# Full-row transposes of x with zeros below the samples, strip 6 transposed inside strip 7, and the last means by token tile

## The chip, the cores and the metric

The kernel runs on one core of a Trainium2 chip. The engines are TensorE (PE; its weight loads are listed apart as PEld), VectorE (DVE), ScalarE (ACT), GpSimd (POOL) and SyncE (SP), which here only issues transfers. The metric is the device time of one execution in microseconds (us), as the median of the runs.

## The reference, cut to what matters

One step of a hybrid streaming encoder in float32, for 256 prompt tokens and 64 sample tokens, each with 2048 features (320 tokens in all):

```
z    = x @ w_in                                   # 2048 -> 7184
mix  = concat(head_rms_norm(attention(z)), head_rms_norm(mLSTM(z)) * sigmoid(o)) @ w_out
x1   = layer_norm(ALPHA * x + mix, ln1_g, ln1_b)
ffn  = (silu(x1 @ w_ffn_gate) * (x1 @ w_ffn_up)) @ w_ffn_down      # 2048 -> 5632 -> 2048
y    = layer_norm(ALPHA * x1 + ffn, ln2_g, ln2_b)
```

layer_norm takes mean and variance of a token over its 2048 features, eps 1e-5. y is an output, tokens in rows. The caches and states that are outputs too lie outside the change.

## The kernel before

**Layout.** Activations are held with features in partitions and tokens in columns: 16 tiles of 128 features by T = 320 tokens. x arrives with tokens in rows, so TensorE transposes it first. `load_x` (L83) brings a quarter q of x (512 features) into a tile `xq` of 128 x 3 x 512: index 0 and 1 of the middle axis hold the 256 prompt tokens, index 2 holds the 64 sample tokens in rows 0 to 63; rows 64 to 127 of it stay as they are. `transpose_x` (L212) makes three transposes for each of the four feature tiles of a quarter, by the list `TOK = [(0, 128), (128, 128), (256, 64)]` of token tiles: the third has 64 rows. Three transposes fill one PSUM tile `w`; ScalarE casts it into a high part `xhi` (L218), VectorE subtracts to get a low part `xlo` (L219).

**Products.** Each weight is cut into a high and a low part too (`split_piece`, L115: ScalarE L130, VectorE L131), and a product is three matmuls: high weight by low x (L180), high by high (L181), low by high (L183). A *strip* is 256 output features, a *piece* is up to four feature tiles by 256 columns of a weight (512 KB). `run_plan` (L158) walks through the list `plan` of pieces; for each of the two 128-column halves of a piece it calls a hook, if one is stored under (piece, half), and then issues the matmuls. A strip's `done` function runs behind its last piece. `spawn` stores a generator that `advance` steps once per piece. The order on each engine is chosen by the framework's scheduler, except for the first eight pieces with the transposes of x (`manual_schedule`) and for instructions given to `keep_in_program_order`. In the first stretch the transposes of quarter 0 stand ahead of piece 0 and of piece 1, quarter 1 ahead of the second half of piece 3, quarter 2 ahead of that of piece 5, quarter 3 ahead of that of piece 7.

**The end.** The last product is `w_ffn_down`, in six groups of up to eight feature tiles; the sixth has four, so a strip there is one piece, two halves of twelve matmuls. `down_done` (L906) adds a strip to the tile y (L912). In the last group each strip but the last also spawns `stat_gen` (L786): six transposes of the strip's two feature tiles back to token rows (L795, 128 columns wide for the two prompt token tiles, 64 wide for the samples), three statistics on VectorE (L797), copies to `ytp` and `yts` by ScalarE (L800, L801), and there a multiplication by the second norm's gain on GpSimd (L803, L805). The generator starts one strip late, so strip 6 is transposed behind strip 7's matmuls; strip 7 follows at once. Then `norm_stats` (L824) joins the statistics to mean and variance, `norm_rsqrt` (L829 to L838) takes the inverse root in small steps on three numbers a row, L1057 to L1065 build a tile `c5` of five columns for each token tile from minus mean times inverse root, TensorE transposes it (L1068), ScalarE casts the three results at once to `r5` (L1070), and twelve matmuls with the gain and bias rows `g5` (L1077), each followed by one VectorE operation (L1078) and a store (L1080), finish y in 512-column parts. The transposes and these twelve share four PSUM tiles `w`.

Of the kernel before, what the change touches and what calls it, by code (L numbers as in the profile page):

```python
# [10 lines left out]
F32R = mybir.dt.float32r  # L11
I32 = mybir.dt.int32
AF = mybir.ActivationFunctionType
ALU = mybir.AluOpType
# [6 lines left out]
P = 128  # L21
DM = 2048
KT = DM // P
SP = 256
SS = 64
T = SP + SS
# [36 lines left out]
def _build(tc, nc, I, O, es):  # L63
# [9 lines left out]
    def w_tile():  # L73
        return pp.tile([P, 512], F32, tag="w", bufs=4, name="w")
# [4 lines left out]
    xq = []  # L79
# [3 lines left out]
    def load_x(q, c0=0, c1=512):  # L83
        if c0 == 0:
            xq.append(big.tile([P, 3, 512], F32, tag="Ba" if q < 2 else "Bb", bufs=2, name="xq"))
        t = xq[q]
        nc.sync.dma_start(out=t[:, 0:2, c0:c1], in_=xp[:, :, q * 512 + c0:q * 512 + c1])
        if c0 == 0:
            nc.sync.dma_start(out=t[0:SS, 2, :], in_=xs[:, q * 512:(q + 1) * 512])
# [47 lines left out]
    def spawn(gen, delay=0):  # L137
        active.append([gen, delay])
# [73 lines left out]
    def transpose_x(q, k0=0, k1=4):  # L212
        for kk in range(k0, k1):
            k = q * 4 + kk
            ps = w_tile()
            for i, (t0, n) in enumerate(TOK):
                TE.transpose(ps[:, t0:t0 + n], xq[q][0:n, i, kk * P:(kk + 1) * P], ident[0:n, 0:n])  # L217
            S.copy(xhi[:, k, :], ps[:, 0:T])  # L218
            V.tensor_tensor(out=xlo[:, k, :], in0=ps[:, 0:T], in1=xhi[:, k, :].bitcast(F32),  # L219
                            op=ALU.subtract)  # L220
# [566 lines left out]
    def stat_gen(s, keep):  # L787


        y, st = late["y"], late["st"]  # L790
        pa, pb = w_tile(), w_tile()
        dst = (pa[:, 0:256], pa[:, 256:512], pb[0:SS, 0:256])
        for j, (t0, n) in enumerate(TOK):
            for i in range(2):
                TE.transpose(dst[j][:, i * P:(i + 1) * P], y[:, 2 * s + i, t0:t0 + n], ident)  # L795
        for j, (t0, n) in enumerate(TOK):
            V.bn_stats(st[0:n, j, s, :], dst[j])  # L797
        if keep is not None:
            cs = slice(s * 256, (s + 1) * 256)
            S.copy(keep[0][:, :, cs], pa.rearrange("p (n c) -> p n c", c=256))  # L800
            S.copy(keep[1][:, cs], dst[2])  # L801
            for j in range(2):
                G.tensor_tensor(out=keep[0][:, j, cs], in0=keep[0][:, j, cs], in1=late["g2"][:, cs],  # L803
                                op=ALU.mult)
            G.tensor_tensor(out=keep[1][:, cs], in0=keep[1][:, cs], in1=late["g2"][0:SS, cs],  # L805
                            op=ALU.mult)
        return
        yield
# [95 lines left out]
    NG = (FT + 7) // 8  # L904

    def down_done(g, s, ps):  # L906
        y = late["y"]
        if g == NG - 1 and s == 0:
            sqrt_table(ps[0][:, 0:1])
        for i in range(2):  # L910
            c = 2 * s + i
            V.scalar_tensor_tensor(out=y[:, c, :], in0=y[:, c, :], scalar=ALPHA if g == 0 else 1.0,  # L912
                                   in1=ps[i][:, 0:T], op0=ALU.mult, op1=ALU.add)
        if g == NG - 1:
            if s == 0:
                late["ytp"] = big.tile([P, 2, DM], F32, tag="A", bufs=2, name="ytp")
                late["yts"] = big.tile([SS, DM], F32, tag="A", bufs=2, name="yts")
            if s < 7:
                spawn(stat_gen(s, (late["ytp"], late["yts"])), 1)

    def gate_up(u):
        rhs = yg_rhs if u < 2 else x1_rhs
# [9 lines left out]
    def down(g):  # L932
        nk = min(8, FT - g * 8)

        def rhs(k):
            return hbuf[("h", g)][:, k, :], hbuf[("l", g)][:, k, :]
        for s in range(8):
            add_strip(I["w_ffn_down"][g * 8 * P:(g * 8 + nk) * P, :], s * 256, 256, rhs,
                      lambda ps, s=s: down_done(g, s, ps), krows=nk)

    for g in range(NG):
        for u in range(g * 4, min(g * 4 + 4, FT // 2)):
            gate_up(u)
        if g > 0:
            down(g - 1)
    down(NG - 1)


    load_x(0, 0, 256)
# [101 lines left out]
    with tc.high_priority():  # L1051
        for _ in stat_gen(7, (late["ytp"], late["yts"])):
            pass
        mv = norm_stats()
        rn = norm_rsqrt(mv)
        nb = lp.tile([P, 3], F32, name="nb")
        V.scalar_tensor_tensor(out=nb, in0=mv[:, :, 0], scalar=-1.0, in1=rn,  # L1057
                               op0=ALU.mult, op1=ALU.mult)

        c5 = lp.tile([P, 3, 5], F32, name="c5")  # L1060
        G.memset(c5, 1.0)
        nbh = lp.tile([P, 3], F32R, name="nbh")
        V.tensor_copy(nbh, nb)
        S.copy(c5[:, :, 0:2], nb.unsqueeze(2).to_broadcast([P, 3, 2]))
        V.tensor_tensor(out=c5[:, :, 2], in0=nb, in1=nbh.bitcast(F32), op=ALU.subtract)  # L1065
        ps = w_tile()
        for j in range(3):
            TE.transpose(ps[0:5, j * P:(j + 1) * P], c5[:, j, :], ident)  # L1068
        r5 = lp.tile([5, 3, P], F32R, name="r5")
        S.copy(r5, ps[0:5, 0:3 * P].rearrange("p (n c) -> p n c", c=P))  # L1070
    for j, (t0, n) in enumerate(TOK):
        v = late["ytp"][:, j, :] if j < 2 else late["yts"]
        dst = O["y_prompt"][t0:t0 + n, :] if j < 2 else O["y_sample"]
# [42 lines left out]
```

## Time and profile before

| | us |
|---|---|
| median of 3 runs (1577.54 to 1581.7) | 1580.44 |
| the profiled execution's own time | 1577.66 |
| its span | 1575.9 |
| TensorE busy | 1561.3 |
| VectorE busy | 835.6 |
| ScalarE busy | 632.4 |
| GpSimd busy | 106.9 |

The profile is of one execution. A row of time order gives the start in us from the span's beginning, the length in us, the engine, the line, the operation with output and inputs, and how many neighbours were merged; in brackets stands the engine's idle time before it and what ended it. A row of a group gives the busy time and the mean of one in ns.

### The profile page before, as it was taken

What the parts mean: (1) busy time and instruction counts of PE and PEld (TensorE: products, weight loads), DVE (VectorE), ACT (ScalarE), POOL (GpSimd) and SP (SyncE); (2) the same over time, 40 slices, a digit from 0 to 9 for tenths busy, and PEclk for the clock granted to TensorE, in tenths of its full rate; (3) what the DMA queues carried; (4) which work ended last, traced back from release to release, by engine and by line L of the source; (5) the groups of instructions that cost most, each with busy time, mean ns of one, the idle gap of its engine ahead of it and who ended that gap; (6) DMA issues with size and microseconds to landing.
All of it is one profiled execution on the core that took longest, in us unless ns stands there. A gap on an engine that the chain in (4) does not pass through costs nothing.

```text
span 1575.9 us, 26646 instructions
## 1 busy us (share of the span) xinstructions
PE 1561.3 (99%) x10924; PEld 1544.1 (98%) x10924; DVE 835.6 (53%) x1529; ACT 632.4 (40%) x969; POOL 106.9 (7%) x249
## 2 busy tenths in 40 slices
PE   9999999999999999999999999999999999999997
PEld 8999999999999999999999999999999999999995
DVE  4486575665865655853344433444335443444456
ACT  4466444454445443643333233323333333333332
POOL 4013101110100000000000000000000000000004
PEclk9999999999999999999999999999999999999997
DMA  8545454444445444445555554444544444444442
GB/s 272 154 147 168 144 161 140 142 150 139 120 136 172 150 147 141 140 148 164 176 162 170 160 162 152 152 147 147 149 153 153 148 147 148 151 148 156 147 134 68
DMA packets 226011, 239.01 MB, mean 152 GB/s; under 512 B 8827, under 2 KB 220475, under 8 KB 225627
## 3 DMA queue, kind: packets, MB, share of 16 engines
q1 hardware_dynamic: 220944, 223.90, 46.0%
q0 software_dynamic: 4944, 13.40, 2.6%
q8 instruction: 86, 1.41, 0.4%
q14 instruction: 37, 0.30, 0.1%
HBM read 230.85 MB, written 10.07 MB: 153 GB/s over the span
## 4 chain that ended last, share of the span: by engine, by line
PE 98%; DVE 1%; issue 0%; ACT 0%; DVEq 0%
PE mm L180 31%; PE mm L181 30%; PE mm L183 30%; PE w L439 1%; PE w L795 1%; PE w L217 1%; PE w L395 0%; PE w L462 0%; PE w L962 0%; PE w L419 0%; DVE ytp L1078 0%; PE w L372 0%; PE w L422 0%; PE w L378 0%; PE w L397 0%; PE w L622 0%
## 5 line engine op out<-in xcount | busy, mean ns | idle before, releaser
L131 DVE TENSOR_TENSOR lo<-raw,hi 128x1024 fp32r<-128x1024 f32 (+1 forms) x410 | 499.0, 1218 | 578.7 <-ACT hi L130 578.2
L130 ACT CAST hi<-raw 128x1024 fp32r<-128x1024 f32 (+1 forms) x410 | 428.3, 1045 | 725.9 <-PE mm L181 636.1
L183 PE MATMUL mm<-x1h,lo 128*128 128x320 f32 (+1 forms) x1408 | 435.5, 309 | 0.0
L181 PE MATMUL mm<-x1h,hi 128*128 128x320 f32 (+1 forms) x1408 | 435.0, 309 | 0.0
L180 PE MATMUL mm<-x1l,hi 128*128 128x320 f32 (+1 forms) x1408 | 434.9, 309 | 0.0
L180 PE MATMUL mm<-xlo,hi 128*128 128x320 f32 x912 | 287.2, 315 | 1.0 <-DVE xlo L219 1.0
L181 PE MATMUL mm<-xhi,hi 128*128 128x320 f32 x912 | 280.7, 308 | 0.0
L183 PE MATMUL mm<-xhi,lo 128*128 128x320 f32 x896 | 277.2, 309 | 0.7 <-DVE lo L131 0.7
L183 PEld LDWEIGHTS mm<-x1h,lo 128*128 128x128 f32 x1408 | 265.3, 188 | 0.0
L180 PEld LDWEIGHTS mm<-x1l,hi 128*128 128x128 f32 x1408 | 265.0, 188 | 0.1
L181 PEld LDWEIGHTS mm<-x1h,hi 128*128 128x128 f32 x1408 | 264.8, 188 | 0.0
L180 PE MATMUL mm<-hl,hi 128*128 128x320 f32 x704 | 218.0, 310 | 0.0
L183 PE MATMUL mm<-hh,lo 128*128 128x320 f32 x704 | 217.6, 309 | 0.0
L181 PE MATMUL mm<-hh,hi 128*128 128x320 f32 x704 | 217.5, 309 | 0.0
L180 PEld LDWEIGHTS mm<-xlo,hi 128*128 128x128 f32 x912 | 171.3, 188 | 1.8 <-ACT hi L130 1.2
L181 PEld LDWEIGHTS mm<-xhi,hi 128*128 128x128 f32 x912 | 171.4, 188 | 0.0
L183 PEld LDWEIGHTS mm<-xhi,lo 128*128 128x128 f32 x896 | 168.2, 188 | 1.2 <-DVE lo L131 1.2
L181 PEld LDWEIGHTS mm<-hh,hi 128*128 128x128 f32 x704 | 132.2, 188 | 0.0
L180 PEld LDWEIGHTS mm<-hl,hi 128*128 128x128 f32 x704 | 132.2, 188 | 0.0
L183 PEld LDWEIGHTS mm<-hh,lo 128*128 128x128 f32 x704 | 132.1, 188 | 0.0
L803 POOL TENSOR_TENSOR ytp<-ytp,g 128x256 f32<-128x256 f32 x16 | 13.6, 871 | 1018.8 <-ACT ytp L800 1018.8
L912 DVE SCALAR_TENSOR_TENSOR y<-y,mm 128x320 f32<-128x320 f32 x96 | 46.4, 483 | 49.0 <-PE mm L183 48.7
(319 smaller groups left out, 1331.2 us busy)
## 6 DMA issues: line engine op xcount, KB each, us to landing
raw<-w_in SPq DMA_DIRECT2D x112, 512.0 KB, 3.6
raw<-w_ffn_gate SPq DMA_DIRECT2D x88, 512.0 KB, 3.5
raw<-w_ffn_up SPq DMA_DIRECT2D x88, 512.0 KB, 3.5
raw<-w_ffn_down SPq DMA_DIRECT2D x88, 512.0 KB, 3.4
raw<-w_out SPq DMA_DIRECT2D x32, 512.0 KB, 3.4
tz<-fdram POOLq DMA_DIRECT2D x16, 144.0 KB, 3.0
u<-cache_attn_k POOLq DMA_DIRECT2D x4, 512.0 KB, 4.0
u<-cache_attn_v POOLq DMA_DIRECT2D x4, 512.0 KB, 6.0
```

Source lines behind the costliest of these rows:

```text
L130: S.copy(hi[:, 0:n], raw[:, 0:n])
L131: V.tensor_tensor(out=lo[:, 0:n], in0=raw[:, 0:n], in1=hi[:, 0:n].bitcast(F32), op=ALU.subtract)
L180: TE.matmul(o, hi[:, sl], xl, start=st, stop=False)
L181: TE.matmul(o, hi[:, sl], xh, start=False, stop=en and pc.perm)
L183: TE.matmul(o, lo[:, sl], xh, start=False, stop=en)
L217: TE.transpose(ps[:, t0:t0 + n], xq[q][0:n, i, kk * P:(kk + 1) * P], ident[0:n, 0:n])
L439: TE.matmul(ox[r, c * 64:(c + 1) * 64], pT[:, j, r], src[:, k, v0:v0 + 64], start=(m == 0), stop=(m == len(terms[c]) - 1))
L795: TE.transpose(dst[j][:, i * P:(i + 1) * P], y[:, 2 * s + i, t0:t0 + n], ident)
L803: G.tensor_tensor(out=keep[0][:, j, cs], in0=keep[0][:, j, cs], in1=late["g2"][:, cs], op=ALU.mult)
L912: V.scalar_tensor_tensor(out=y[:, c, :], in0=y[:, c, :], scalar=ALPHA if g == 0 else 1.0, in1=ps[i][:, 0:T], op0=ALU.mult, op1=ALU.add)
```

## The change

Four edits:

- `load_x` sets rows 64 to 127 of the third part of `xq` to zero on VectorE, and `transpose_x` transposes all 128 rows of each part, three whole 128x128 transposes. The 64 surplus columns land in the PSUM tile behind the 320 that are read.
- A hook ahead of the second half of the last piece (`last_strip`) runs strip 6's `stat_gen` there and then the addition of strip 7's first half (`down_add`), which `down_done` no longer does.
- For strip 7, `stat_gen` makes no copies and no GpSimd multiplications; the PSUM tiles are kept, and after `c5` VectorE multiplies them by the gain straight into `ytp` and `yts`. In `stat_gen` the loop over the two feature tiles is now the outer one, for every strip of both layer norms.
- The cast to `r5` is made for each token tile right behind its transpose.

The diff:

```diff
--- before.py
+++ after.py
@@ -83,6 +83,8 @@
     def load_x(q, c0=0, c1=512):
         if c0 == 0:
             xq.append(big.tile([P, 3, 512], F32, tag="Ba" if q < 2 else "Bb", bufs=2, name="xq"))
+
+            V.memset(xq[q][SS:P, 2, :], 0.0)
         t = xq[q]
         nc.sync.dma_start(out=t[:, 0:2, c0:c1], in_=xp[:, :, q * 512 + c0:q * 512 + c1])
         if c0 == 0:
@@ -213,8 +215,8 @@
         for kk in range(k0, k1):
             k = q * 4 + kk
             ps = w_tile()
-            for i, (t0, n) in enumerate(TOK):
-                TE.transpose(ps[:, t0:t0 + n], xq[q][0:n, i, kk * P:(kk + 1) * P], ident[0:n, 0:n])
+            for i in range(3):
+                TE.transpose(ps[:, i * P:(i + 1) * P], xq[q][:, i, kk * P:(kk + 1) * P], ident)
             S.copy(xhi[:, k, :], ps[:, 0:T])
             V.tensor_tensor(out=xlo[:, k, :], in0=ps[:, 0:T], in1=xhi[:, k, :].bitcast(F32),
                             op=ALU.subtract)
@@ -790,12 +792,16 @@
         y, st = late["y"], late["st"]
         pa, pb = w_tile(), w_tile()
         dst = (pa[:, 0:256], pa[:, 256:512], pb[0:SS, 0:256])
-        for j, (t0, n) in enumerate(TOK):
-            for i in range(2):
-                TE.transpose(dst[j][:, i * P:(i + 1) * P], y[:, 2 * s + i, t0:t0 + n], ident)
+        for i in range(2):
+            for j, (t0, n) in enumerate(TOK):
+                t = TE.transpose(dst[j][:, i * P:(i + 1) * P], y[:, 2 * s + i, t0:t0 + n], ident)
+                if keep is not None and s == 7:
+                    tc.keep_in_program_order(t)
         for j, (t0, n) in enumerate(TOK):
             V.bn_stats(st[0:n, j, s, :], dst[j])
-        if keep is not None:
+        if keep is not None and s == 7:
+            late["last"] = dst
+        elif keep is not None:
             cs = slice(s * 256, (s + 1) * 256)
             S.copy(keep[0][:, :, cs], pa.rearrange("p (n c) -> p n c", c=256))
             S.copy(keep[1][:, cs], dst[2])
@@ -904,19 +910,28 @@
     NG = (FT + 7) // 8
 
     def down_done(g, s, ps):
-        y = late["y"]
         if g == NG - 1 and s == 0:
             sqrt_table(ps[0][:, 0:1])
         for i in range(2):
-            c = 2 * s + i
-            V.scalar_tensor_tensor(out=y[:, c, :], in0=y[:, c, :], scalar=ALPHA if g == 0 else 1.0,
-                                   in1=ps[i][:, 0:T], op0=ALU.mult, op1=ALU.add)
+            if (g, s, i) != (NG - 1, 7, 0):
+                down_add(g, s, i, ps)
         if g == NG - 1:
             if s == 0:
                 late["ytp"] = big.tile([P, 2, DM], F32, tag="A", bufs=2, name="ytp")
                 late["yts"] = big.tile([SS, DM], F32, tag="A", bufs=2, name="yts")
-            if s < 7:
+            if s < 6:
                 spawn(stat_gen(s, (late["ytp"], late["yts"])), 1)
+
+    def last_strip():
+
+        for _ in stat_gen(6, (late["ytp"], late["yts"])):
+            pass
+        down_add(NG - 1, 7, 0, plan[-1].group["ps"])
+
+    def down_add(g, s, i, ps):
+        y, c = late["y"], 2 * s + i
+        V.scalar_tensor_tensor(out=y[:, c, :], in0=y[:, c, :], scalar=ALPHA if g == 0 else 1.0,
+                               in1=ps[i][:, 0:T], op0=ALU.mult, op1=ALU.add)
 
     def gate_up(u):
         rhs = yg_rhs if u < 2 else x1_rhs
@@ -944,6 +959,7 @@
         if g > 0:
             down(g - 1)
     down(NG - 1)
+    hooks[(len(plan) - 1, 1)] = last_strip
 
 
     load_x(0, 0, 256)
@@ -1063,11 +1079,16 @@
         V.tensor_copy(nbh, nb)
         S.copy(c5[:, :, 0:2], nb.unsqueeze(2).to_broadcast([P, 3, 2]))
         V.tensor_tensor(out=c5[:, :, 2], in0=nb, in1=nbh.bitcast(F32), op=ALU.subtract)
+        cs = slice(7 * 256, DM)
+        for j, (t0, n) in enumerate(TOK):
+            v = late["ytp"][:, j, cs] if j < 2 else late["yts"][:, cs]
+            tc.keep_in_program_order(V.tensor_tensor(out=v, in0=late["last"][j],
+                                                     in1=late["g2"][0:n, cs], op=ALU.mult))
         ps = w_tile()
+        r5 = lp.tile([5, 3, P], F32R, name="r5")
         for j in range(3):
             TE.transpose(ps[0:5, j * P:(j + 1) * P], c5[:, j, :], ident)
-        r5 = lp.tile([5, 3, P], F32R, name="r5")
-        S.copy(r5, ps[0:5, 0:3 * P].rearrange("p (n c) -> p n c", c=P))
+            S.copy(r5[:, j, :], ps[0:5, j * P:(j + 1) * P])
     for j, (t0, n) in enumerate(TOK):
         v = late["ytp"][:, j, :] if j < 2 else late["yts"]
         dst = O["y_prompt"][t0:t0 + n, :] if j < 2 else O["y_sample"]
```

Lines behind L83 count two more in the new kernel, those near the end 6 to 21 more (L1078 is L1099 there). Three places show how the order moves. In the rows of the built program, `w` is the PSUM tile, `mm` the tile of the products, and a size is the output's.

TensorE at the front, from the nine matmuls that run while x is on its way to the first product; before:

```order
L962 MATMUL w<-idle 128x128 x9
L217 MATMUL w<-ident,xq 128x128 x2
L217 MATMUL w<-ident,xq 128x64
L217 MATMUL w<-ident,xq 128x128 x2
L217 MATMUL w<-ident,xq 128x64
L180 MATMUL mm<-xlo,hi 128x320
```

and now:

```order
L978 MATMUL w<-idle 128x128 x9
L219 MATMUL w<-ident,xq 128x128 x6
L182 MATMUL mm<-xlo,hi 128x320
L183 MATMUL mm<-xhi,hi 128x320
L185 MATMUL mm<-xhi,lo 128x320
```

The count of transposes is the same; the third of each three has the full width now. The other groups of x's transposes change alike.

VectorE from the last strip on; before (y the additions, `st` the statistics, `mv` mean and variance, the small tiles the steps of the inverse root, `c` the tile `c5`):

```order
L912 SCALAR_TENSOR_TENSOR y<-y,mm 128x320 x2
L797 BN_STATS st<-w 128x6 x4
L797 BN_STATS st<-w 64x6
L824 BN_AGGR mv<-st 128x2 x2
L797 BN_STATS st<-w 64x6
L824 BN_AGGR mv<-st 64x2
L831 TENSOR_SCALAR rnh<-mv 128x3
```

and now:

```order
L933 SCALAR_TENSOR_TENSOR y<-y,mm 128x320
L801 BN_STATS st<-w 128x6 x2
L801 BN_STATS st<-w 64x6
L933 SCALAR_TENSOR_TENSOR y<-y,mm 128x320
L801 BN_STATS st<-w 128x6 x2
L801 BN_STATS st<-w 64x6
L830 BN_AGGR mv<-st 128x2 x2
L830 BN_AGGR mv<-st 64x2
L837 TENSOR_SCALAR rnh<-mv 128x3
```

Three of the six statistics behind the last addition now stand ahead of it. Between `c5` and the first operation of L1099 three multiplications are new (L1085).

TensorE behind the last product; before:

```order
L795 MATMUL w<-ident,y 128x128 x4
L795 MATMUL w<-ident,y 64x128
L795 MATMUL w<-ident,y 128x128 x4
L795 MATMUL w<-ident,y 64x128 x3
L1068 MATMUL w<-ident,c_15927 5x128 x3
L1077 MATMUL w<-g_5986,r_15937 128x512 x12
```

and now:

```order
L797 MATMUL w<-ident,y 128x128 x2
L797 MATMUL w<-ident,y 64x128
L797 MATMUL w<-ident,y 128x128 x2
L797 MATMUL w<-ident,y 64x128
L1090 MATMUL w<-ident,c_15926 5x128 x2
L1098 MATMUL w<-g_5990,r_15936 128x512 x2
L1090 MATMUL w<-ident,c_15926 5x128
L1098 MATMUL w<-g_5990,r_15936 128x512 x10
```

Twelve transposes of y behind the last product are six now, the other six stand ahead of the last twelve matmuls; the transposes of `c5` are split, two ahead of the first product with `g5` and one between the second and the third.

## The prediction

> **What bounds the kernel now.** I read the page's first part and its chain of waits, then the weight loads of TensorE in order of time, because the edit touches two places only: the transposes of x in the first 36 us and the work behind the last strip.
>
> ```profile
> span 1575.9 us, 26646 instructions
> PE 1561.3 (99%) x10924; PEld 1544.1 (98%) x10924; DVE 835.6 (53%) x1529; ACT 632.4 (40%) x969; POOL 106.9 (7%) x249
> PE 98%; DVE 1%; issue 0%; ACT 0%; DVEq 0%
> ```
>
> TensorE is busy 1561.3 of 1575.9 us and makes up 98% of the chain that ended last. So a microsecond of TensorE time saved anywhere ahead of the last matmul moves everything behind it, unless a transfer or a cast at that place is late already. Behind the last matmul the chain is VectorE's, and there only what stands on that chain counts.
>
> **The start: transposes of x.** Columns of these rows: start, length, engine, line and operation; an x count merges neighbours.
>
> ```profile
> 15.30 0.19 PEld L183 LDWEIGHTS mm<-xhi,lo 128*128 128x128 f32 x1
> 15.44 0.29 PEld L217 LDWEIGHTS w<-ident,xq 128*128 128x128 f32 x2
> 15.89 0.40 PEld L217 LDWEIGHTS w<-ident,xq 64*128 64x128 f32 x3 [0.17 <-issue]
> ...
> 17.81 0.19 PEld L180 LDWEIGHTS mm<-xlo,hi 128*128 128x128 f32 x1
> ...
>   issue: 2.8, 16
> ...
> 74.08 0.50 PEld L419 LDWEIGHTS w<-ident,u 128*128 128x128 f32 x4
> ...
> 75.32 0.30 PEld L394 LDWEIGHTS w<-kT,qbd 128*128 128x128 f32 x2
> ```
>
> Each 64-row load (the 64 sample tokens) stands 0.17 us behind its predecessor with nothing to wait for; the row "issue: 2.8, 16", from the answer on the tile of x, adds that up over all sixteen. Twelve transposes of one quarter of x occupy the array from 15.44 to 17.81: 2.37 us, 0.20 each. Eleven transposes with all 128 rows (eight 128 columns wide, three 64) run from 74.08 to 75.32: 1.24 us, 0.113 each, twelve therefore 1.36. The gap per quarter is 1.0 us, more than the four pauses (0.68). The change makes all of x's transposes 128-row, so I price them like those of line 419: 1.0 us off each of the quarters 1, 2 and 3, and half of it, 0.5, off the second half of quarter 0.
>
> The first half of quarter 0 is not TensorE's to win, since a chain of casts follows it:
>
> ```profile
> 6.10 0.43 ACT L218 CAST xhi<-w 128x320 fp32r<-128x320 f32 x1 [4.01 <-PE w L217]
> ...
> 6.55 1.09 DVE L219 TENSOR_TENSOR xlo<-w,xhi 128x320 fp32r<-128x320 f32 x2 [5.45 <-ACT xhi L218]
> ...
> 8.42 0.41 PE L183 MATMUL mm<-xhi,lo 128*128 128x320 f32 x1 [0.17 <-DVE lo L131]
> ```
>
> The cast at 6.10 can start earlier by the pause ahead of the third transpose and a little of its load, 0.25 us (between 0 and 0.35), VectorE's operation at 6.55 follows it, and the matmul at 8.42 waits for VectorE and moves with it. Sum for the start: 0.25 + 0.5 + 3 x 1.0 = **3.75 us**. The lower bound takes only the pauses, 14 x 0.17 = 2.4, the upper 4.0.
>
> Is the work there to run earlier? The tightest place is piece 4, which TensorE reaches right behind quarter 1:
>
> ```profile
> 0.91 0.17 DVE L94 MEMSET idle<- 128x128 f32 x1 [0.91 <-PEq L1104]
> ...
> 13.61 1.05 ACT L130 CAST hi<-raw 128x1024 fp32r<-128x1024 f32 x1 [1.48 <-DMA raw<-w_in]
> ...
> 14.70 1.23 DVE L131 TENSOR_TENSOR lo<-raw,hi 128x1024 fp32r<-128x1024 f32 x1 [1.84 <-ACT hi L130]
> 16.66 2.21 DVE L219 TENSOR_TENSOR xlo<-w,xhi 128x320 fp32r<-128x320 f32 x4 [0.74 <-ACT xhi L218]
> ...
> 25.16 2.21 DVE L219 TENSOR_TENSOR xlo<-w,xhi 128x320 fp32r<-128x320 f32 x4 [3.47 <-ACT xhi L218]
> ```
>
> Its weights land at 13.6, its low part is done at 15.93, and the four low parts of x (0.55 each) can then end at 18.15. With 1.75 us gained TensorE starts piece 4 at 16.94 instead of 18.69 (17.81 plus six matmuls at 0.147 us, the step from the load at 15.30 to that at 15.44), and wants the four at 16.9, 17.4, 17.8 and 18.25: they arrive at 16.5, 17.05, 17.6 and 18.15. It just fits; 0.3 us lost here is my allowance, inside the lower bound. The next quarters have room: the 3.47 us that VectorE idles ahead of 25.16.
>
> The zero-filling is four 64x512 memsets on VectorE. Three stand at its front, where it is idle until 6.55, the fourth ahead of the idle stretch just named. The nearest row is the memset of 128x128 at 0.91, 0.17 us; four times the columns is at most 0.7 each, 2.1 for three, over by about 3.2. Cost 0; without that cover 2.8. In the built program no transfer of x waits for them, only TensorE's third transpose of a tile does.
>
> **The end: strip 6 inside strip 7.**
>
> ```profile
> 1546.17 0.70 PEld L795 LDWEIGHTS w<-ident,y 128*128 128x128 f32 x6
> ...
> 1554.87 0.49 DVE L912 SCALAR_TENSOR_TENSOR y<-y,mm 128x320 f32<-128x320 f32 x1 [1.27 <-PE mm L183]
> ...
> 1557.91 0.36 DVE L824 BATCH_NORM_AGGREGATE mv<-st 64x2 f32<-64x48 f32 x1
> ...
> 621.25 0.70 PEld L795 LDWEIGHTS w<-ident,y 128*128 128x128 f32 x6
> ...
> 622.03 1.09 DVE L797 BATCH_NORM_STATS2 st<-w 128x6 f32<-128x256 f32 x3 [1.32 <-PE w L795]
> 623.04 0.81 DVE L824 BATCH_NORM_AGGREGATE mv<-st 128x2 f32<-128x48 f32 x3
> ```
>
> Six transposes cost 0.70 us of TensorE. They now stand ahead of the last twelve matmuls, so the last addition moves from 1554.87 to 1555.57 and ends at 1556.06. Behind it stood six statistics and three means, done at 1558.27 (1557.91 and 0.36); now there are three and three. The first layer norm shows what these take: the first statistic 0.45 behind the load of the fourth transpose (621.59), and 1.82 from it to the last mean (622.03 to 623.85). The fifth transpose loads at 1556.2, so the statistics start at 1556.65 and the means are done at 1558.47. **Loss 0.2 us** for this part alone.
>
> **The end: no GpSimd.**
>
> ```profile
> 1556.83 2.77 POOL L803 TENSOR_TENSOR ytp<-ytp,g 128x256 f32<-128x256 f32 x4 [2.05 <-ACT ytp L800]
> 1559.55 1.40 POOL L805 TENSOR_TENSOR yts<-yts,g 64x256 f32<-64x256 f32 x2
> ...
> 1558.30 0.30 ACT L829 ACTIVATE sd<-mv,eps 128x3 f32<-128x3 f32 x1
> ...
> 1558.30 0.63 DVE L831 TENSOR_SCALAR rnh<-mv 128x3 f32<-128x3 f32 x1
> ...
> 1559.05 0.56 DVE L836 TENSOR_TENSOR rna<-rn 128x3 f32<-128x3 f32 x1
> ...
> 1561.00 0.16 DVE L1057 SCALAR_TENSOR_TENSOR nb<-mv,rn 128x3 f32<-128x3 f32 x1
> ...
> 625.11 0.16 DVE L836 TENSOR_TENSOR rna<-rn 128x3 f32<-128x3 f32 x1
> 625.30 0.16 DVE L837 TENSOR_TENSOR rna<-rna,rnh 128x3 f32<-128x3 f32 x1
> ```
>
> The same operation on three numbers takes 0.16 us at 625 and 0.56 here. GpSimd works without a break from 1556.83 to 1560.95, and the slow ones end when one of its six does (the one of 1559.05 at 1559.61, GpSimd's fourth at 1559.60); the first after 1560.95 takes 0.16 again. I read it as VectorE waiting for GpSimd. In the changed kernel GpSimd has only strip 6, whose three operations now come ahead of the last twelve matmuls, so 12 x 0.147 = 1.76 us sooner: from about 1555.1, at 0.7 each, to 1557.2, ahead of the small operations (the cover is 1.2 us). Then the root of ScalarE (0.30) and four steps at 0.19 (625.11 to 625.30) lead from 1558.47 to the start of line 1057's operation at 1559.65 instead of 1561.00: **1.35 us** gained, the 0.2 already paid.
>
> **The end: means by token tile.**
>
> ```profile
> 1561.78 0.80 PE L1068 MATMUL w<-ident,c 128*5 128x128 f32 x3 [5.49 <-DVE c L1065]
> ...
> 1562.62 0.47 ACT L1070 CAST r<-w 5x384 fp32r<-5x384 f32 x1 [1.17 <-PE w L1068]
> ...
> 1563.14 7.11 PE L1077 MATMUL w<-g,r 5*128 5x512 f32 x12 [0.56 <-ACT r L1070]
> ...
> 1564.05 5.36 DVE L1078 SCALAR_TENSOR_TENSOR ytp<-ytp,rn,w 128x512 f32<-128x512 f32 x8 [2.41 <-PE w L1077]
> ...
> L868 DVE TENSOR_TENSOR np<-mm,r 128x320 f32<-128x320 f32 x8 | 3.7, 482 | 0.0
> ```
>
> From 1561.78 to the first product of line 1077 pass 1.36 us. Now a single transpose (a third of 0.80, 0.27), a cast of a third of the columns (between 0.16 and 0.47, taken 0.3), and the second transpose (0.27), which the order puts ahead of the products, stand there, with the two handovers of about 0.05: 0.95. Gain **0.4 us**, between 0.1 and 0.65. The twelve final operations stay bound by VectorE at 0.67 each (5.36 for eight). The three new multiplications read PSUM; 0.48 for 320 columns bounds each, 1.45 together, and they stand in VectorE's idle 2.41 us, of which 2.0 are left. Cost 0; that cover gone, they would cost up to 1.45.
>
> The end gives 1.35 + 0.4 = **1.75 us** (1.2 to 2.0). **Sum**: 3.75 + 1.75 = 5.5 us. The profiled execution took 1577.66 us, so it would take 1572.2. Its time lies near the fastest of the three runs shown (1577.54), the median is 1580.44; against that the same gain gives **1574.9**, which I forecast.
>
> **The rivals.** *Only the pauses go* (2.4 at the start, or a stall at piece 4): 2.4 + 1.75 = 4.15, 1576.3. For it: the pause is all that the row names; against it: the 0.113 of line 419.
> *GpSimd is not the cause* of the slow small operations: the end then gives 0.4 - 0.2 = 0.2, the sum 3.95, 1576.5. Against it speaks that the delays end with GpSimd's operations.
> *The loads pace the start*: what TensorE gains it waits again for weights, as ScalarE does at 13.61. Only the end is left, 1.75, 1578.7. Against it: no later cast in these rows waits for a transfer.
> *The new order of the strips' transposes costs* (slower). Before, four 128-column loads are followed by two 64-column ones; now they alternate, in all sixteen strips of both layer norms, two more changes of shape in each. If such a change paused the array like the 64-row ones, 32 x 0.17 = 5.4 us would eat the gain, and with a pause half as long again, 8.2, the kernel would be slower: 1583.1; it decides from 0.17 on. Against it:
>
> ```profile
> 69.46 0.29 PEld L372 LDWEIGHTS w<-ident,vT 128*128 128x128 f32 x2
> 69.71 0.11 PEld L373 LDWEIGHTS w<-ident,vT 128*64 128x64 f32 x1
> ...
> 70.15 0.47 PEld L378 LDWEIGHTS w<-ident,u 128*128 128x128 f32 x4
> ```
>
> Here six loads alternate just so and take 0.69 us (69.46 to 70.15), as long as the grouped six at 1546.17 (0.70). By the Trainium skill, "TensorEngine Tiling (Array Packing)", Key Properties, changing the tiling mode drains the array, and it lists 128x64 as a mode of its own beside 64x128; by that rule this rival would hold. The trace agrees for 64 rows (0.17 us) and not for 64 columns (0.69 against 0.70), and I follow the trace.
>
> **How the numbers follow.** Forecast 0.60; only the pauses 0.15; GpSimd not the cause 0.10; loads pace the start 0.10; slower 0.05. Runs shown spread from 1577.54 to 1581.7, so 0.3%, 4.7 us, is about what a measurement can tell from none. The forecast's 5.5 lies 0.8 above that, so I give it three chances in four of showing (0.45), the next two a third each (0.08): faster 0.53, slower 0.04, else the same. Range: the fastest run less the highest sum (4.0 + 2.0) gives 1571.5; the slowest less 2.7 (the lower end of the third rival with a little of the start) gives 1579.0; I take 1571 to 1579. The likeliest case alone holds 1572 to 1577.
>
> **What would show it.** In the profile after: no idle "issue" time ahead of the loads of x, twelve of them in about 1.4 us; the first matmul behind quarter 3 near 32 instead of 35.68; the small operations behind the means at 0.16 each; VectorE's first operation of line 1099 1.75 us closer to the last strip's addition than it was, corrected for the 0.70. Wrong would be an idle TensorE ahead of piece 4, a 64-column load with idle time, or small operations still at 0.6 with GpSimd at rest.

## The result, and the profile after

The changed kernel takes 1572.66 us (median of four runs, 1571.77 to 1573.35), the kernel before, run beside it, 1581.07 (four runs, 1577.54 to 1581.70): a ratio of 0.9949, interval 0.9934 to 0.9965. It is faster, by 5.5 to 10.4 us. Sixty further executions of the kernel before have a median of 1578.6, so the gain is nearer 6 than 8. The profiled execution took 1573.34 us, against 1577.66 before.

The page of the changed kernel, first part:

```profile
span 1571.6 us, 26652 instructions
PE 1558.3 (99%) x10924; PEld 1544.3 (98%) x10924; DVE 836.3 (53%) x1536; ACT 631.0 (40%) x969; POOL 105.0 (7%) x246
```

The span is 4.3 us shorter, and TensorE's busy time 3.0. The number of matmuls is the same; their rows at the front tell why. Changed kernel, weight loads of TensorE in order of time (start, length, engine, line, operation; in brackets the idle time ahead and its end):

```profile
5.62 0.42 PEld L219 LDWEIGHTS w<-ident,xq 128*128 128x128 f32 x4 [0.75 <-issue]
...
8.15 0.29 PEld L185 LDWEIGHTS mm<-xhi,lo 128*128 128x128 f32 x1 [0.43 <-DVE lo L133]
8.32 0.34 PEld L182 LDWEIGHTS mm<-xlo,hi 128*128 128x128 f32 x1
8.59 0.33 PEld L183 LDWEIGHTS mm<-xhi,hi 128*128 128x128 f32 x1
...
10.73 0.89 PEld L219 LDWEIGHTS w<-ident,xq 128*128 128x128 f32 x6
...
15.94 1.38 PEld L219 LDWEIGHTS w<-ident,xq 128*128 128x128 f32 x12
17.29 0.19 PEld L182 LDWEIGHTS mm<-xlo,hi 128*128 128x128 f32 x1
...
23.42 1.38 PEld L219 LDWEIGHTS w<-ident,xq 128*128 128x128 f32 x12
...
33.12 0.19 PEld L182 LDWEIGHTS mm<-xlo,hi 128*128 128x128 f32 x1
```

Twelve transposes are one row of 1.38 us without a pause; from its start to the next load are 1.35 (15.94 to 17.29), against 2.37 before. But the rows from 8.15 to 10.73 hold something that the profile of before did not show: the matmuls of piece 0 stand 0.267 us apart, not 0.147. TensorE runs at half its speed there, until within the transposes at 10.73: its granted clock is 0.50 from 7.7 to 11.1, and 1.00 on either side. The load behind quarter 3 stands at 33.12; before:

```profile
35.68 0.19 PEld L180 LDWEIGHTS mm<-xlo,hi 128*128 128x128 f32 x1
```

That is 2.56 us earlier, of which the half speed has taken its part.

The end of the changed kernel on VectorE:

```profile
1552.99 0.49 DVE L933 SCALAR_TENSOR_TENSOR y<-y,mm 128x320 f32<-128x320 f32 x1 [0.79 <-PE mm L185]
1554.01 1.08 DVE L801 BATCH_NORM_STATS2 st<-w 128x6 f32<-128x256 f32 x3 [0.53 <-PE w L797]
1555.03 0.80 DVE L830 BATCH_NORM_AGGREGATE mv<-st 128x2 f32<-128x48 f32 x3
1555.86 0.17 DVE L837 TENSOR_SCALAR rnh<-mv 128x3 f32<-128x3 f32 x1
...
1556.40 0.16 DVE L842 TENSOR_TENSOR rna<-rn 128x3 f32<-128x3 f32 x1
...
1556.99 0.16 DVE L1073 SCALAR_TENSOR_TENSOR nb<-mv,rn 128x3 f32<-128x3 f32 x1
...
1557.85 0.76 DVE L1085 TENSOR_TENSOR ytp<-w,g 128x256 f32<-128x256 f32 x2 [0.23 <-issue]
1558.52 0.41 DVE L1085 TENSOR_TENSOR yts<-w,g 64x256 f32<-64x256 f32 x1
1559.69 5.48 DVE L1099 SCALAR_TENSOR_TENSOR ytp<-ytp,rn,w 128x512 f32<-128x512 f32 x8 [0.77 <-PE w L1098]
```

and on GpSimd, its last operation:

```profile
1554.00 0.72 POOL L811 TENSOR_TENSOR yts<-yts,g 64x256 f32<-64x256 f32 x1
```

From the last addition to the first final operation are 6.70 us, against 9.18 before (1554.87 to 1564.05). The small operations take 0.16 or 0.17 each, GpSimd has ended at 1554.72, before the first of them, and the three new multiplications stand in a gap of which 0.77 us are still idle. Of the 2.48 us, 0.70 are only moved: strip 6's transposes now lie ahead of the last addition. The end's own gain is 1.78.

### The profile page after: what moved, and what is told of

Read it like the earlier page. It is cut to its first block, busy times and chain, and to the rows that moved or that the text cites. A ratio compares the mean times of both kernels' runs of the same rounds, so it can differ in the third digit from the quotient of the medians.

```text
span 1571.6 us, 26652 instructions
## 1 busy us (share of the span) xinstructions
PE 1558.3 (99%) x10924; PEld 1544.3 (98%) x10924; DVE 836.3 (53%) x1536; ACT 631.0 (40%) x969; POOL 105.0 (7%) x246
## 4 chain that ended last, share of the span: by engine, by line
PE 98%; DVE 1%; DMA 0%; issue 0%; ACT 0%; DVEq 0%; SPq 0%
PE mm L182 31%; PE mm L183 31%; PE mm L185 31%; PE w L441 1%; PE w L797 1%; PE w L397 0%; PE w L219 0%; PE w L464 0%; DMA xq<-x_sample 0%; DVE ytp L1099 0%; PE w L421 0%; PE w L374 0%; PE w L424 0%; PE w L380 0%; PE w L399 0%; PE w L624 0%
```

## The experiments

Twelve runs were made, of ten kernels. Times are medians; a ratio is to the kernel before on the same chip. In the first four, each part of the change stands alone, the kernel before is run against itself, and the half speed is attacked.

### The kernel before against itself

No edit.

> The kernel before, unchanged, for a second profile and more times: its runs lay between 1577.5 and 1581.7 us, those of the changed kernel between 1571.8 and 1573.4. Theory 'front speed': executions differ by how long TensorE runs at half speed in the first 12 us, so a profile of a slower run shows matmuls of line 181 at about 0.27 us apart instead of 0.147 in some stretch before 15 us, worth the difference (up to 4 us), and the rest of the span alike. Rival 'spread elsewhere': the front is alike and the difference lies in the middle of the span or at the stores.

1578.63 us (1577.77 to 1581.61, 11 runs), ratio 0.9999 [0.9990, 1.0007]. The profiled execution took 1578.82 and differs from the first one at the front, as the weight loads show:

```profile
8.52 0.33 PEld L181 LDWEIGHTS mm<-xhi,hi 128*128 128x128 f32 x1
8.79 0.33 PEld L183 LDWEIGHTS mm<-xhi,lo 128*128 128x128 f32 x1
...
36.84 0.19 PEld L180 LDWEIGHTS mm<-xlo,hi 128*128 128x128 f32 x1
```

Here the same kernel runs piece 0 at 0.267 us a matmul, and the load behind quarter 3 comes 1.16 us later than at 35.68; the last addition (1556.04) too comes 1.17 later, and the distance behind it is 9.18 again. So TensorE's speed at the front differs between executions of one and the same kernel; the change is not needed for it. Like must be compared with like: at half speed, 36.84 before and 33.12 after, 3.72 us.

### The transposes alone

```diff
 # the kernel before
+            V.memset(xq[q][SS:P, 2, :], 0.0)
-            for i, (t0, n) in enumerate(TOK):
-                TE.transpose(ps[:, t0:t0 + n], xq[q][0:n, i, kk * P:(kk + 1) * P], ident[0:n, 0:n])
+            for i in range(3):
+                TE.transpose(ps[:, i * P:(i + 1) * P], xq[q][:, i, kk * P:(kk + 1) * P], ident)
```

> The kernel before with the 128-row transposes of x and the zeros alone; the end is the old one. Theory (prediction): 3.75 us of the gain are here, ratio 0.9976; in the profile twelve transposes in 1.4 us, and the last addition (line 912) earlier by 2.5 to 3.8 us, the lower figure if piece 0 runs at half speed. Rival 'the loads pace the start': the ratio is 1.000 and TensorE idles ahead of some piece before 40 us.

1573.49 us (1573.32 to 1574.92, 5 runs), ratio 0.9966 [0.9953, 0.9978]. Its profile fell on full speed, and can be laid beside the profile of before:

```profile
8.03 0.19 PEld L185 LDWEIGHTS mm<-xhi,lo 128*128 128x128 f32 x1 [0.43 <-DVE lo L133]
...
9.46 0.72 PEld L219 LDWEIGHTS w<-ident,xq 128*128 128x128 f32 x6
10.15 0.19 PEld L182 LDWEIGHTS mm<-xlo,hi 128*128 128x128 f32 x1
...
14.52 1.37 PEld L219 LDWEIGHTS w<-ident,xq 128*128 128x128 f32 x12
15.86 0.19 PEld L182 LDWEIGHTS mm<-xlo,hi 128*128 128x128 f32 x1
...
31.69 0.19 PEld L182 LDWEIGHTS mm<-xlo,hi 128*128 128x128 f32 x1
```

The load at 8.03 stood at 8.42: 0.39. Quarter 0's second half takes 0.69 (9.46 to 10.15) instead of 1.23: 0.54. Quarters 1 to 3 take 1.34 or 1.35 instead of 2.36 or 2.37: 3.07. Together 4.0, and the last row shows it: 31.69 instead of 35.68, 3.99. From the end of quarter 1's transposes to the start of quarter 2's pass 6.13 us in this kernel, in the changed one (17.29 to 23.42) and in the kernel before: no transfer and no cast holds TensorE up on the way.

### The end alone

```diff
 # the changed kernel
-            V.memset(xq[q][SS:P, 2, :], 0.0)
-            for i in range(3):
-                TE.transpose(ps[:, i * P:(i + 1) * P], xq[q][:, i, kk * P:(kk + 1) * P], ident)
+            for i, (t0, n) in enumerate(TOK):
+                TE.transpose(ps[:, t0:t0 + n], xq[q][0:n, i, kk * P:(kk + 1) * P], ident[0:n, 0:n])
```

> The changed kernel with the old 64-row transposes of x: the end alone. Theory (prediction): 1.75 us gained between the last addition and the first final operation, after paying 0.70 for the six transposes ahead of the last twelve matmuls; ratio 0.9989. Rival 'GpSimd is not the cause': 0.2 us, ratio 0.9999. The sum of this gain and that of the rows alone should be that of the whole change, 0.9949.

1577.15 us (1576.08 to 1580.06, 11 runs), ratio 0.9990 [0.9981, 0.9999]: 1.4 us by the medians. In its profile the first final operation stands 6.97 behind the last addition, 1.51 us gained net of the 0.70 (7.06 and 1.42 in its second profile, the last run below). The two parts' ratios multiply to 0.9956, inside the whole's interval: as far as these intervals reach, they add.

### More work for TensorE at the front

```diff
 # the changed kernel
-        for _ in range(9):
+        for _ in range(11):
             TE.matmul(warm[:, 0:P], idle, idle, start=True, stop=True)
         transpose_x(0, 0, 2)
+        for _ in range(6):
+            TE.matmul(warm[:, 0:P], idle, idle, start=True, stop=True)
```

> The changed kernel with 11 instead of 9 idle matmuls ahead of the transposes and six more behind the first six transposes, where TensorE idled from 6.1 to 7.4 us. Theory 'front speed': the idle time let TensorE fall to half speed for the twelve matmuls of piece 0 (0.267 apart in the profile after); kept busy it runs them at 0.147, and the kernel gains up to 1.3 us: 1571.4 to 1571.8 in all runs, the spread of 1.6 us gone. Rival 'late data': piece 0 is slow for another reason (its operands' arrival), the twelve stay at 0.267 and the time stays 1572 to 1573.4.

1572.87 us (1572.05 to 1573.04, 5 runs), ratio 0.9959 [0.9945, 0.9972]. The profile shows piece 0 at full speed and the load behind quarter 3 at 31.72. The times are no better than the changed kernel's; the extra matmuls are no improvement that can be measured, and none of the five runs reached the 1571.4 to 1571.8 that the theory expected of all. That the idle time is what brings the half speed is not shown by this: a third of the executions of the kernel before fall into the group whose profiles run piece 0 at full speed without the extra matmuls (last section).

### GpSimd kept busy

```diff
 # the changed kernel, in stat_gen behind the two multiplications by the gain
+            if s == 6:
+                for j in range(5):
+                    G.tensor_tensor(out=late["scr"], in0=keep[0][:, j % 2, cs],
+                                    in1=late["g2"][:, cs], op=ALU.mult)
```

> The changed kernel with five more GpSimd multiplications behind strip 6's, at 0.7 us each, so that GpSimd works to about 1558.3 (strip 6's end at 1554.7 in the profile after) while VectorE does the small operations behind the means (1555.8 to 1557.2 there). The five write only a scratch tile, so the result stays the reference's. Theory (GpSimd's running operations hold the small ones up): those at L837 to L844 and L1078 take 0.5 to 0.65 us instead of 0.16, each ending with one of GpSimd's, and the first final operation comes about 1.3 us farther behind the last addition than in the changed kernel (6.70 there), so near 8.0. Rival (the slowness before had to do with what GpSimd worked on, or with the time of day in the kernel, not with GpSimd's being busy): the small operations stay at 0.16 and the distance at 6.7.

One execution (1573.4 us). VectorE:

```profile
1554.76 0.36 DVE L841 TENSOR_SCALAR rnh<-mv 128x3 f32<-128x3 f32 x1
1555.09 0.18 DVE L843 RECIPROCAL rn<-sd 128x3 f32<-128x3 f32 x1
1555.30 0.61 DVE L846 TENSOR_TENSOR rna<-rn 128x3 f32<-128x3 f32 x1
1555.94 0.16 DVE L847 TENSOR_TENSOR rna<-rna,rnh 128x3 f32<-128x3 f32 x1
1556.14 0.57 DVE L848 SCALAR_TENSOR_TENSOR rn<-rna,rn 128x3 f32<-128x3 f32 x1
...
1556.95 0.58 DVE L1084 CAST nbh<-nb 128x3 fp32r<-128x3 f32 x1
...
1559.87 5.48 DVE L1104 SCALAR_TENSOR_TENSOR ytp<-ytp,rn,w 128x512 f32<-128x512 f32 x8 [1.07 <-PE w L1103]
```

and GpSimd, four of the five:

```profile
1554.37 0.72 POOL L815 TENSOR_TENSOR scr<-ytp,g 128x256 f32<-128x256 f32 x1
...
1555.17 0.72 POOL L815 TENSOR_TENSOR scr<-ytp,g 128x256 f32<-128x256 f32 x1
...
1555.97 0.72 POOL L815 TENSOR_TENSOR scr<-ytp,g 128x256 f32<-128x256 f32 x1
...
1556.78 0.73 POOL L815 TENSOR_TENSOR scr<-ytp,g 128x256 f32<-128x256 f32 x1
```

The slow operations are back, and each ends with one of GpSimd's: at 1555.12, 1555.91, 1556.71 and 1557.53, where GpSimd's end at 1555.09, 1555.89, 1556.69 and 1557.51. The distance from the last addition (1551.89) is 7.98 us instead of 6.70, as expected (near 8.0). That GpSimd's running operations hold VectorE's up is shown by this. GpSimd's own stand 0.80 apart here and 0.68 before the change, but that is not VectorE's doing: the first two are 0.79 apart already (1553.58 and 1554.37), while VectorE works on the statistics and the means. The five write one scratch tile.

Not every operation is held. Two with two inputs take 0.16 (at 1555.94 and 1556.75): each starts 0.05 or 0.06 us behind the end of one of GpSimd's, which leave gaps of 0.07 or more here. In the kernel before they leave none, and such an operation right behind a held one is held again (0.65 at 1559.64); the reciprocal in that place takes 0.16 (1558.85). Here it takes 0.18, and the statistics, which read PSUM, had their usual 1.08 for three at 1552.91, while GpSimd worked. The Trainium skill, "SBUF — State Buffer", Who interferes with whom, says that the two engines share one pair of memory ports, held by one of them for a whole instruction, and that VectorE needs it with two inputs from SBUF or in a two-port mode, which a scalar operation and a cast can enter. The traces agree: held were operations with two inputs, the scalar operation and the cast, not the reciprocal.

### The cast to `r5` at once

```diff
 # the changed kernel
         for j in range(3):
             TE.transpose(ps[0:5, j * P:(j + 1) * P], c5[:, j, :], ident)
-            S.copy(r5[:, j, :], ps[0:5, j * P:(j + 1) * P])
+        S.copy(r5, ps[0:5, 0:3 * P].rearrange("p (n c) -> p n c", c=P))
```

> The changed kernel with the cast to r5 made at once behind the third transpose of c5, as before the change. Theory: the first final operation comes 0.35 us later behind nb (2.70 in the profile after, 3.05 before), since two transposes and two thirds of a cast return to the path: 3.05 here. Rival (the 0.35 came from elsewhere, the order of the products or the smaller wait for a PSUM tile): 2.7 to 2.8.

One execution (1572.3 us). VectorE:

```profile
1555.85 0.16 DVE L1073 SCALAR_TENSOR_TENSOR nb<-mv,rn 128x3 f32<-128x3 f32 x1
...
1558.89 5.35 DVE L1099 SCALAR_TENSOR_TENSOR ytp<-ytp,rn,w 128x512 f32<-128x512 f32 x8 [1.11 <-PE w L1098]
```

From `nb` to the first final operation are 3.04 us, against 2.70 in the changed kernel: the split is worth 0.34 there. Two more profiles with the split have 2.71 and 2.72 (little work at the front, and the old order, both below); the end alone and the kernel with more work at the front have 2.98 to 3.07 (the next section comes back to them). Not all of the 0.34 reaches the end. With the third transpose between the products, eight final operations take 5.48 us; without it 5.35; and from the last addition to the end of the span are 18.75 here and 18.6 in the changed kernel. By this pair 0.15 us of the 0.34 are kept; but the two profiles of the end alone, one kernel, differ by 0.21 in that distance (18.60 and 18.81), so what is kept is not shown clear of that.

The changed kernel's rows show what the split costs on TensorE:

```profile
1557.77 0.37 PE L1090 MATMUL w<-ident,c 128*5 128x128 f32 x1 [3.68 <-DVE c L1081]
1558.48 0.38 PE L1090 MATMUL w<-ident,c 128*5 128x128 f32 x1 [0.34 <-ACT r L1091]
1558.79 1.22 PE L1098 MATMUL w<-g,r 5*128 5x512 f32 x2
```

The second transpose waits for the first cast, which reads the same PSUM tile.

### The old order of the strips' transposes

```diff
 # the changed kernel, stat_gen: token tile outside again for all strips but the last
-        for i in range(2):
-            for j, (t0, n) in enumerate(TOK):
+        for i, (j, (t0, n)) in ([(i, jt) for i in range(2) for jt in enumerate(TOK)]
+                                if keep is not None and s == 7 else
+                                [(i, jt) for jt in enumerate(TOK) for i in range(2)]):
```

> The changed kernel with the old order (token tile outside, feature tile inside) of the strips' transposes in all strips but the last, so that the 128-column loads stand together again, as before the change. Theory: the alternation with 64-column loads costs nothing; six transposes take 0.70 either way, the time is that of the changed kernel, 1572.7, within 0.5 us. Rival (each change of shape pauses the array): two changes fewer in fifteen strips; at the 0.17 us of the 64-row loads 5 us less, 1567.6, and idle time ahead of the 64-column loads of the changed kernel that goes here.

1572.07 us (1571.51 to 1572.14, 5 runs), ratio 0.9955 [0.9941, 0.9969], not to be told from the changed kernel's (0.6 below its median, where the theory allowed 0.5; the changed kernel's own runs spread over 1.6). Strips of the last group, here and in the changed kernel:

```profile
1546.27 0.70 PEld L799 LDWEIGHTS w<-ident,y 128*128 128x128 f32 x6
```

```profile
1547.81 0.69 PEld L797 LDWEIGHTS w<-ident,y 128*128 128x128 f32 x6
```

Six loads take 0.70 grouped and 0.69 alternating. The rival of 5 us is gone: a change in the number of columns costs nothing here.

### The 64-row transposes grouped

```diff
 # the kernel before, transpose_x
-            for i, (t0, n) in enumerate(TOK):
-                TE.transpose(ps[:, t0:t0 + n], xq[q][0:n, i, kk * P:(kk + 1) * P], ident[0:n, 0:n])
+            pss.append(ps)
+            for i in range(2):
+                TE.transpose(ps[:, i * P:(i + 1) * P], xq[q][:, i, kk * P:(kk + 1) * P], ident)
+        for kk in range(k0, k1):
+            k, ps = q * 4 + kk, pss[kk - k0]
+            TE.transpose(ps[:, SP:T], xq[q][0:SS, 2, kk * P:(kk + 1) * P], ident[0:SS, 0:SS])
```

> The kernel before with the transposes of x grouped within each quarter: the full-row ones of all its feature tiles first, then the 64-row ones together. Same count, same shapes, no zeros. Theory A (the pause belongs to the change from 128 to 64 rows): one pause a quarter instead of four, twelve transposes in 1.6 to 1.8 us instead of 2.37, so some 2 us less over the four quarters: 1576.5 against 1578.6. Theory B (each 64-row load costs its pause, whatever stands before it): four pauses a quarter, 2.3 us, the time that of the kernel before. In both, the casts of a quarter start a little later, since no feature tile is complete until the second group begins (0.3 us at most, ahead of piece 0 on the path).

1575.67 us (1574.86 to 1577.31, 10 runs), ratio 0.9981 [0.9972, 0.9991]. Quarter 1:

```profile
15.30 0.94 PEld L218 LDWEIGHTS w<-ident,xq 128*128 128x128 f32 x8
16.41 0.32 PEld L221 LDWEIGHTS w<-ident,xq 64*128 64x128 f32 x4 [0.17 <-issue]
16.80 0.19 PEld L180 LDWEIGHTS mm<-xlo,hi 128*128 128x128 f32 x1
```

One pause instead of four, and 1.50 us instead of 2.37 for the same twelve transposes: theory A, and more than the 1.6 to 1.8 us that it expected. The price belongs to the change of rows: three changes to 64 rows and back fewer save 0.87, 0.29 each, of which the pause in the row is only 0.17. Reordering alone wins 2.9 us by the medians; the zeros win 0.15 more a quarter, and perhaps half a microsecond ahead of piece 0, where the grouped kernel's load stands at 8.57 and that of the transposes alone at 8.03; but the kernel before itself has 8.07, 8.08 and 8.42 there in its three profiles. The rule that the prediction drew on (the Trainium skill, "TensorEngine Tiling (Array Packing)", Key Properties) holds by this trace for rows, and by the one above not for columns.

### Little work for TensorE at the front, after and before

```diff
 # the changed kernel, and apart from it the kernel before
-        for _ in range(9):
+        for _ in range(1):
             TE.matmul(warm[:, 0:P], idle, idle, start=True, stop=True)
```

> The changed kernel with one idle matmul at the front instead of nine, so that TensorE has done almost nothing when the first transposes of x come. Theory (the front's speed sets the spread of the times; half speed costs more where the 64-row pauses stretch it): piece 0 and quarter 0's transposes run at half speed in every execution (matmuls 0.267 us apart instead of 0.147), piece 0 is 1.1 us longer, and the time is 1 to 2 us above the changed kernel's 1572.7, without runs beyond 1575. Rival (idle matmuls have no effect on the speed): the time is that of the changed kernel.

1574.13 us (1572.81 to 1574.24, 5 runs), ratio 0.9967 [0.9954, 0.9980], 1.5 above the changed kernel, as the theory had it. In its one profile (1573.56) piece 0 and the first transposes behind it run at half speed:

```profile
10.76 0.33 PEld L185 LDWEIGHTS mm<-xhi,lo 128*128 128x128 f32 x1
11.03 0.91 PEld L219 LDWEIGHTS w<-ident,xq 128*128 128x128 f32 x6
```

It is not a stretch that sets in later, as in the changed kernel: the first transposes of x are slow already (the four at 5.58 take 0.71, where the changed kernel's at 5.62 take 0.42).

> The kernel before with one idle matmul at the front instead of nine. Theory (the slow executions of the kernel before, 1580.3 to 1581.7, are those in which TensorE is at half speed at the front for longer): the time moves up to them, 1580 to 1582 in nearly all runs, and the profile shows half speed beyond quarter 0's second transposes. Rival (those slow executions come from something else): the median rises by the 1.1 us of piece 0 at most, and the spread of 4 us stays.

1578.82 us (1578.61 to 1581.19, 10 runs), ratio 0.9998 [0.9989, 1.0008]. The theory expected 1580 to 1582 in nearly all runs; one of ten came there, so it fell. What vanished is the lower end: no run under 1578.6, where the kernel before has a third of its runs at 1577.5 to 1578.0. The spread shrank from 4 us to 2.6.

### Two more profiled executions

The kernel before, and the kernel with the end alone, unchanged.

> The kernel before, unchanged, for one more profiled execution. Theory (the two lower groups of its times differ in TensorE's speed in piece 0): a time of 1577.5 to 1578.0 comes with the matmuls of piece 0 0.147 us apart, one of 1578.4 to 1578.9 with 0.267. A time of 1580.3 to 1581.7 would show by its rows where the further 2.8 us lie; if they too are TensorE's speed at the front, half speed lasts beyond 12.3 there and the last addition comes at 1557.6 or later. Rival: the groups show no such difference at the front.

1578.56 us. Weight loads:

```profile
8.33 0.19 PEld L181 LDWEIGHTS mm<-xhi,hi 128*128 128x128 f32 x1
8.48 0.23 PEld L183 LDWEIGHTS mm<-xhi,lo 128*128 128x128 f32 x1
8.65 0.33 PEld L180 LDWEIGHTS mm<-xlo,hi 128*128 128x128 f32 x1
8.92 0.33 PEld L181 LDWEIGHTS mm<-xhi,hi 128*128 128x128 f32 x1
```

> The changed kernel with the old 64-row transposes of x, unchanged from its earlier run, for one more profiled execution. Theory: a time of 1576.0 to 1576.4 comes with piece 0 at full speed (0.147 us apart), one of 1576.9 to 1577.4 with half speed (0.267), as 1577.15 did. One of 1578.9 to 1580.1 would show where the further 2.8 us lie: half speed beyond 12.3 by the theory, elsewhere by the rival.

1576.15 us, with piece 0 at 0.147 us a matmul throughout and the load behind quarter 3 at 35.80.

Both came as the theory had it: half speed with the middle group of times (here it sets in within piece 0, at 8.6), full speed with the lowest. Neither fell on the slowest times.

## Why the prediction was right, and where not

**Forecast.** 1574.9 us, 1571 to 1579, faster as the likeliest: measured 1572.66, faster. The 2.2 us between the two numbers come from the base (below), not from the sum: the same sum taken from the profiled execution gave 1572.2.

**The sum of 5.5.** Right when like is laid beside like. Both at half speed: 1578.82 before (the second profile) and 1573.34 after are 5.5 apart, 3.72 of it at the load behind quarter 3.

**The base: the step that failed.** I put the gain on the median of the three runs shown, 1580.44, although the profiled execution (1577.66) gave 1572.2. The sixty later executions show that two of those three lay in the upper groups of its times (last section) and that the median is 1578.6. "Against that the same gain" was wrong too: 17 of the 60 took 1580.3 or more, while none of 24 runs of kernels with full-row transposes (the changed kernel, the transposes alone, more and little work at the front, the old order of the strips) lies more than 1.6 us above the fastest of its kernel. So the first comparison shows 8.4 by its medians and the later ones about 6.

**The start, 3.75.** Measured 3.99 at full and 3.72 at half speed. By terms at full speed: first half of quarter 0 0.25 forecast, 0.39 measured in the kernel with the transposes alone; second half 0.5 and 0.54; quarters 1.0 and 1.01 to 1.03. At half speed the quarters are the same, but the first half gives nothing (the load stands at 8.08 before and 8.15 after) and the second 0.73, so that the sum comes so near to 3.75 there is partly luck. The first term is the loosest, and 0.39 is one pair: at full speed the load of 8.42 stands from 7.94 to 8.38 in the kernels with full rows, in the kernel before it stands at 8.07 and 8.08 in the other two profiles, and one of the waits there is not the pause that I took it for. In the changed kernel TensorE's third transpose starts 0.54 late for the transfer of the samples (TensorE's own row names it; the load at 5.62 shows 0.75 as "issue"). Pricing by line 419's loads rather than by the pauses was right, and grouping the rows shows why: the pause is 0.17, the change of rows costs 0.29. Piece 4 fits, with no idle TensorE ahead of it; the memsets took 0.5 each in VectorE's idle time.

**The end, 1.75.** Measured 1.78 at the first final operation, 1.51 in the kernel with the end alone. The means are done 2.84 behind the last addition instead of 3.40: with the 0.70 that is a loss of 0.14, forecast 0.2. `nb` comes 4.00 behind it instead of 6.13, 1.43 gained net where 1.35 stood. (The root and the four steps named for the way from the means to `nb` make 1.06 of the 1.18 that stood in the prediction; measured are 1.16.) The token tiles give 0.35 (forecast 0.4), and that is where a size was off: by the pair with the single cast only about 0.15 of it outlives the final operations, where the third transpose stands between the products. Counted from the last addition to the end of the span, six profiles with the new end have 18.5 to 18.9 us and three of the kernel before 20.9 to 21.0, by the means 1.6 gained net of the 0.70. In the kernel with the end alone nearly 0.4 us more pass between the first product and the first final operation, in both its profiles (1.28 and 1.26 instead of 0.90): VectorE starts there 0.06 and 0.04 us behind the end of the second product, not behind the first. In the one with more work at the front `c` starts 0.46 late, so that its distance is 7.05. Why is open in both.

**The rivals.** Only the pauses: refuted (3.7 to 4.0 at the start, not 2.4). GpSimd not the cause: refuted by keeping it busy. Loads pace the start: refuted, 6.13 us from quarter 1 to quarter 2 in all three profiles laid side by side. The strips' order: refuted, 0.70 against 0.69.

**What was to be seen.** The signs came but for two. Idle "issue" time was to be gone ahead of all loads of x; it is gone except for the 0.75 at 5.62, which is the transfer just named. And the load behind quarter 3 was to be near 32 and stood at 33.12, because of the half speed; in the five full-speed profiles with full rows it stands at 31.60 to 32.03.

## What to carry to other kernels

A 64-row transpose between 128-row ones cost more here than the idle time ahead of it showed (0.29 against 0.17 us); pad the rows with zeros, or group the odd shapes, and price the edit from a stretch of equal shapes. Keep GpSimd at rest while VectorE works through a chain of small operations on SBUF. Before adding a gain to a median, look whether the runs fall into groups, and lay profiles of the same group side by side.

## What the runs showed of the hardware

TensorE's speed at the front differs from one execution to the next. The 60 executions of the kernel before fall into four groups with gaps between them, and in the first three the mean granted clock goes with the time: 1577.5 to 1578.0 at a clock of 0.995 (20 runs), 1578.4 to 1578.9 at 0.994 (23), 1580.3 to 1580.6 at 0.993 (10). The fourth, 1581.6 to 1581.8 (7), has 0.995 again. Profiles of the first two groups show full speed in piece 0, or half. Four profiles have half speed behind nine idle matmuls: the changed kernel's, two of the kernel before, one of the end alone. In each the granted clock is 0.50 for 3.4 us, from 7.7, 8.1, 8.6 and 8.8 on. An estimate from these two figures: 1.7 us of work at full speed are lost, 0.001 of 1577, which is the step in the mean clock.

The third group would then have two such stretches; that is argued, since no profile fell on it. The fourth has the full clock, and its 3.9 us are unexplained. Both are missing in the 24 runs with full-row transposes. With 64-row ones they are there in the end alone too (three of 11 runs at 1578.9 with 0.993, one at 1580.06 with 0.995), and the ten runs with the 64-row ones grouped have the fourth's like alone (two at 1577.31, clock 0.995).

The mean clock tells executions of one kernel apart, not kernels. With one idle matmul at the front the matmuls of piece 0 stand 0.267 apart and the granted clock still reads 1.00 there: the record does not count the half speed that TensorE has from its start, and those runs have 0.995 or 0.996.

The Trainium skill, "TensorE: Matmul & The Clock Gate", What's actually happening, describes a clock set by activity in windows of about 3.4 us that run on regardless of the kernel, so that the count of slow matmuls varies from run to run; the four stretches agree in length, and their differing starts (7.7 to 8.8) do as well.

TensorE's wait of 1.2 to 1.4 us for the first casts, ahead of piece 0, was in all profiles but that with more work at the front. What decides whether half speed follows it is not shown. The matmuls that the kernel issues ahead of x do have a part: with one instead of nine the lowest group disappeared.
